# Making scale and shift together, so that the first projections of a hybrid attention block run on final inputs

## The chip, the cores and the metric

The kernel runs on one core of a Trainium2 chip. The metric is the device time of one execution, in microseconds (us), as the median of several runs. Beside the runs there is one profiled execution, with a trace of every instruction and every DMA packet. The engines are called PE (matrix products and transposes by matmul), DVE (vector), ACT (activation), POOL (GpSimd) and SP (which here only issues DMAs). DMAs can be issued from the queues of SP, ACT and POOL.

## The reference, cut to what matters

One block of a model with two branches (window attention and a gated linear recurrence). All numbers are float32. Only the first lines concern the change: 256 tokens of `x` and 256 tokens of context `ctx`, of width 2048, are normalized, scaled and shifted, and then multiplied by column groups of `w_in`.

```python
mod = silu(c) @ w_ada + b_ada                       # c: (1, 2048), w_ada: (2048, 6144)
shift, scale, gate = split(mod[:, None, :], 3, axis=-1)
mod_c = silu(c_ctx) @ w_ada + b_ada                 # the same for the context
shift_c, scale_c, gate_c = split(mod_c, 3, axis=-1)
xn = rmsnorm(x, norm_gain) * (1.0 + scale) + shift
cn = rmsnorm(ctx, norm_gain) * (1.0 + scale_c) + shift_c
... = split_columns(xn @ w_in)                      # aq ak av ag hq hff hfb hi hg ma mb
... = split_columns(cn @ w_in)
f = lb + (1 - lb) * sigmoid(z)                      # z: columns hff and hfb, forget gates
... # recurrence over hq, f, hi; window attention over aq, ak, av; gates; two output products
h = x + gate * ((sigmoid(ma + b0) * y_hgrn + sigmoid(mb + b1) * y_att) @ w_out)
return rmsnorm(h, final_norm_gain)
```

## The kernel before, in words

Every large product is done with float32 split in two parts: `wchunk` (L67) loads a piece of a weight matrix of 128 x 1024 elements into a raw buffer (`wload`, L59, issued on SP's queue), rounds it to a high part on ACT (L74, tile wh) and takes the rest on DVE (L75, tile wl). The inputs are kept likewise, as `xH` and `xL` (two halves of the tile xHL). `mm3` (L80) then makes three matmuls, high x high (L81), high x low (L82) and low x high (L83). The width 2048 is cut in KT = 16 tiles of 128, the 512 tokens (x and context) in four tiles of 128.

The opening, which the change is about, goes up to the values of the first heads:

- Small rows (c, c_ctx, biases, gains, bounds) are loaded on SP's and ACT's queues, turned by PE into columns (`cT`, `cols`).
- `turn_x` (L277) takes the sum of squares of each token tile, makes the factor 1/rms (`rstd_of`, L175, on POOL), scales the rows of X by it (L291 on ACT, L293 on DVE), and turns X in blocks of 128 x 128 on PE (L298; copied back by L300 and L302).
- `modulation(s, k, n)` (L306) makes scale (s = 1) or shift (s = 0) for n tiles from tile k on, for both c and c_ctx: `contract` (L185) runs 16 narrow matmuls (tile pa, L196) in four column strips of PE over loads of w_ada of 512 KB, ACT copies the sums (L201), PE turns them (tq, L205), DVE adds the strips (L208) and the bias (L317 or L320, L322).
- `scaled(kt)` (L332) makes xH and xL of a tile with the scale only. `first_pieces` (L368) runs the first projections on these: three groups of 256 columns of w_in (the first forget gates: C_FF, C_FB, C_FF + 256), 18 matmuls a tile, into six banks that stay open for all 16 tiles (tiles pj and pf).
- The units of scale are 2, 4, 4, 4, 2 tiles (`UNITS`, L403). In the table `plan` (L417) the steps of the next scale unit and of the shift units (`shift`, L416: three of four) are put between the pieces of the first projections.
- Behind them `shifted(kt)` (L341) makes xH and xL anew with scale and shift for 12 tiles, the six banks are copied out raw (L439, L441), and the projection HI of all four token tiles runs (`proj_tok_g`, L88). Into its steps are put the last shift unit, `shifted` for the last four tiles, and `shift_bias` (L382), which multiplies the shift with the first projections' weights, loaded again, to get what the raw banks lack (`biasF`).
- After HI, `token_values` (L753, lines L759 and L761) copies its banks out, `forget` (L478) makes the gates from the raw banks and biasF (L487 ACT, L488 DVE), and the projection HQ begins (`proj_col_x_g`, L128; its matmuls are L139 and L144).

The order on PE and SP in the opening is the order of the program (`manual_schedule`, L405); that of the other engines is fixed when the kernel is built, by priorities. Loads of the opening go to a ring of eight raw buffers (pool st), the chunks of `wchunk` to one of four, and their split parts to three pairs.

## Time and profile before

| | |
|---|---|
| median of 3 runs | 1673.35 us (1673.25 to 1674.57) |
| profiled execution, own time | 1670.86 us |
| its span in the trace | 1669.1 us |
| PE busy | 1633.2 us (98%) |
| DVE, ACT, POOL busy | 980.4, 754.0, 24.7 us |
| granted clock of PE | 0.999 |
| bytes moved by DMA | 280.45 MB, 168 GB/s over the span |

A line of a group in the profile reads: line of the kernel, engine, operation, out<-in by the program's names, shapes, count, then busy us in total and mean ns of one, then idle time of the engine just before, and what ended it. In a timeline a row is start us, duration us, engine, line, operation, operands, and in brackets the idle time before it and who ended it. Matmuls overlap, so the distance between starts is what one costs, not its duration.

### The profile page before, as it was taken

Reading aid. Unit: us, or ns where it says so; the run is one execution under the profiler, and the core shown is the slowest. Engines: PE = TensorE matmul, PEld = TensorE weight load, DVE = VectorE, ACT = ScalarE, POOL = GpSimd, SP = SyncE. Lnnn points to the kernel's source line nnn. Section 1 sums busy time; section 2 is a strip of 40 time slices with the busy share of each in tenths; the row PEclk is TensorE's granted clock in tenths of the full one; section 3 lists DMA queues with packets and bytes.
Section 4 is the critical chain, followed back from the end, with each engine's and each line's share of the span. In section 5 each row is a group of like instructions: output and inputs, shape, how many; then the busy total and the mean of one; then the engine's idle time right before and its main releaser. Section 6 shows DMA issues by size and latency. Waiting matters only on the chain.

```text
span 1669.1 us, 22846 instructions
## 1 busy us (share of the span) xinstructions
PE 1633.2 (98%) x8945; PEld 1345.0 (81%) x8945; DVE 980.4 (59%) x1533; ACT 754.0 (45%) x1125; POOL 24.7 (1%) x80
## 2 busy tenths in 40 slices
PE   5999999999999999999999999999999999999997
PEld 3657788888888888888888888888888888788887
DVE  4445577546666375754667555334677676555665
ACT  5333544324443243433445443223576777444443
POOL 1000000000000000000000000000000000000000
PEclk9999999999999999999999999999999999999999
DMA  9897654336343453434435565434545455666554
GB/s 346 309 337 259 232 168 127 114 99 213 104 128 112 132 187 107 130 106 152 141 100 171 172 196 193 141 99 132 174 137 153 138 161 158 202 202 190 180 181 139
DMA packets 182189, 280.45 MB, mean 168 GB/s; under 512 B 8961, under 2 KB 89153, under 8 KB 181313
## 3 DMA queue, kind: packets, MB, share of 16 engines
q1 hardware_dynamic: 180480, 275.70, 51.5%
q0 software_dynamic: 672, 2.11, 0.5%
q8 instruction: 70, 1.15, 0.3%
q10 hardware_dynamic: 928, 1.18, 0.2%
q14 instruction: 39, 0.31, 0.1%
HBM read 276.86 MB, written 2.10 MB: 167 GB/s over the span
## 4 chain that ended last, share of the span: by engine, by line
PE 94%; DVE 2%; DMA 1%; ACT 0%; issue 0%; SPq 0%; POOLq 0%; POOL 0%; ACTq 0%; DVEq 0%
PE pj L81 24%; PE pj L83 24%; PE pj L82 24%; PE pj L139 7%; PE pj L144 3%; PE al L567 2%; PE pa L196 1%; DMA raw<-in_w_ada_dram 1%; PE tkp L994 1%; PE sb L643 1%; DVE wl L75 0%; PE sc L83 0%; PE sc L81 0%; PE sc L82 0%; PE oba L83 0%; PE oba L81 0%
## 5 line engine op out<-in xcount | busy, mean ns | idle before, releaser
L75 DVE TENSOR_TENSOR wl<-raw,wh 128x1024 fp32r<-128x1024 f32 x396 | 484.4, 1224 | 459.1 <-ACT wh L74 458.5
L74 ACT ACTIVATE wh<-raw 128x1024 fp32r<-128x1024 f32 x396 | 419.0, 1058 | 604.4 <-PE pj L83 384.4
L83 PE MATMUL pj<-wh,xHL 128*128 128x512 f32 (+1 forms) x1024 | 397.0, 388 | 0.0
L82 PE MATMUL pj<-wl,xHL 128*128 128x512 f32 (+1 forms) x1024 | 395.8, 387 | 0.4 <-DVE wl L75 0.4
L81 PE MATMUL pj<-wh,xHL 128*128 128x512 f32 (+1 forms) x1024 | 393.1, 391 | 0.0
L81 PEld LDWEIGHTS pj<-wh,xHL 128*128 128x128 f32 x1024 | 192.3, 188 | 41.0 <-issue 3.0
L83 PEld LDWEIGHTS pj<-wh,xHL 128*128 128x128 f32 x1024 | 192.4, 188 | 39.7 <-issue 0.7
L82 PEld LDWEIGHTS pj<-wl,xHL 128*128 128x128 f32 x1024 | 192.6, 188 | 38.3 <-DVE wl L75 0.7
L81 PE MATMUL pj<-xHL,wh 128*128 128x512 f32 x480 | 191.1, 398 | 3.3 <-ACT xHL L338 3.2
L83 PE MATMUL pj<-xHL,wl 128*128 128x512 f32 x480 | 187.5, 391 | 1.8 <-DVE wl L75 1.8
L82 PE MATMUL pj<-xHL,wh 128*128 128x512 f32 x480 | 187.4, 390 | 0.0
L139 PE MATMUL pj<-xHL,wh 128*128 128x512 f32 x512 | 181.6, 398 | 1.1 <-DVE v L759 1.1
L144 PE MATMUL pj<-xHL,wl 128*128 128x256 f32 x512 | 139.9, 283 | 0.0
L139 PEld LDWEIGHTS pj<-xHL,wh 128*128 128x128 f32 x512 | 95.2, 188 | 20.8 <-DVE v L759 1.3
L81 PEld LDWEIGHTS pj<-xHL,wh 128*128 128x128 f32 x480 | 90.1, 188 | 25.7 <-ACT xHL L338 3.9
L83 PEld LDWEIGHTS pj<-xHL,wl 128*128 128x128 f32 x480 | 90.1, 188 | 21.7 <-DVE wl L75 2.6
L82 PEld LDWEIGHTS pj<-xHL,wh 128*128 128x128 f32 x480 | 90.2, 188 | 18.4 <-DVE xHL L339 0.7
L82 PE MATMUL pj<-wl,bH 128*128 128x512 f32 x256 | 100.0, 390 | 0.0
L83 PE MATMUL pj<-wh,bL 128*128 128x512 f32 x256 | 99.7, 390 | 0.0
L144 PEld LDWEIGHTS pj<-xHL,wl 128*128 128x128 f32 x512 | 96.7, 189 | 2.5
L81 PE MATMUL pj<-wh,bH 128*128 128x512 f32 x256 | 89.9, 391 | 0.1
L610 DVE TENSOR_TENSOR A<-A,X 128x512 f32<-128x512 f32 x96 | 62.0, 688 | 11.7 <-ACT qk L546 10.9
(245 smaller groups left out, 1638.3 us busy)
## 6 DMA issues: line engine op xcount, KB each, us to landing
raw<-in_w_in_dram SPq DMA_DIRECT2D x300, 512.0 KB, 3.6
raw<-in_w_ada_dram SPq DMA_DIRECT2D x96, 512.0 KB, 6.2
raw<-in_w_o_hgrn_dram SPq DMA_DIRECT2D x32, 512.0 KB, 4.1
raw<-in_w_o_attn_dram SPq DMA_DIRECT2D x32, 512.0 KB, 3.7
raw<-in_w_out_dram SPq DMA_DIRECT2D x32, 512.0 KB, 4.2
raw<-in_w_in_dram SPq DMA_DIRECT2D x32, 256.0 KB, 6.7
X<-in_x_dram SPq DMA_DIRECT2D x2, 1024.0 KB, 9.1
X<-in_ctx_dram SPq DMA_DIRECT2D x2, 1024.0 KB, 13.0
```

Source lines behind the costliest of these rows:

```text
L74: act.activation(h[:, :n], raw[:, :n], AF.Copy)
L75: dve.tensor_tensor(lo[:, :n], raw[:, :n], h[:, :n].bitcast(F32), op=ALU.subtract)
L81: pe.matmul(o, s[0], m[0], start=first, stop=False)
L82: pe.matmul(o, s[0], m[1], start=False, stop=False)
L83: pe.matmul(o, s[1], m[0], start=False, stop=last)
L139: pe.matmul(banks[i].rearrange("p (a t) -> p a t", a=2), h[:, j, cs_], xHL[:, :, kt, :T], start=kt == 0, stop=kt == KT - 1)
L144: pe.matmul(banks[i][:, :T], lo[:, j, cs_], xH[:, kt, :T], start=False, stop=False)
L196: pe.matmul(pa[32 * g: 32 * g + 32, :w], lhs[:, k0 + g, :], mv[g], start=k0 == 0, stop=k0 == KT - 4, tile_position=(0, 32 * g))
L567: pe.matmul(o, ky, mv, start=True, stop=True, tile_position=(0, 64 * c))
L610: dve.tensor_tensor(av, av, f.unsqueeze(3).to_broadcast([P, 2, n2, b]), op=ALU.mult)
L643: pe.matmul(o, wT[:, 4 * d + 2 * i + s, :], vc[:, s, (2 * p + i) * HD: (2 * p + i + 1) * HD], start=s == 0, stop=s == 1)
L994: pe.transpose(tk[:, q, :], prs[n][:, q * P: (q + 1) * P], ident)
```

## The change

Small rows go to POOL's queue, and the four loads of X come first on SP's. `turn_x` turns X unscaled; the factors 1/rms are spread over all partitions by one matmul with ones (`spread_rs`) and multiplied in later. `contract`, `scaled`, `shifted`, `shift_bias` and the raw copies are gone. `modulation(k, n)` makes scale and shift of n tiles in one go, in units of 1, 1, 2, 2, ... 2 tiles; the loads of w_ada have 128 columns for a unit of one tile and 256 for one of two. `modulate(kt)` makes the final xH and xL from X, scale, spread factors and shift. The first projections then run on these, and `forget` reads their banks directly, before HI. Between the first steps PE gets idle transposes (`rest`). The diff, cut to its core:

```diff
-    def contract(lhs, load, w, rp):
...
         with tc.high_priority(3 * PRIO):
+            for i in range(4):
+                nc.sync.dma_start(X[:, i, :], (x if i < 2 else cx)[(i % 2) * P: (i % 2 + 1) * P, :])
             nc.scalar.dma_start(cs[:, :P], cst[:, :P])
+            nc.gpsimd.dma_start(crow[0:16, :], c.rearrange("o (r p) -> (o r) p", p=P))
...
+        nc.gpsimd.dma_start(rows[0:32, :], b_ada[0:4096].rearrange("(r p) -> r p", p=P))
+        nc.gpsimd.dma_start(rows[32:48, :], rv(norm_gain))
+        nc.gpsimd.dma_start(rows2[0:32, :], lb_f.rearrange("d (r p) -> (d r) p", p=P))
+        nc.gpsimd.dma_start(rows2[32:64, :], lb_b.rearrange("d (r p) -> (d r) p", p=P))
+        nc.gpsimd.dma_start(rows2[64:80, :], rv(hg_gain))
...
+        dgx = base.tile([P, 512], F32, tag="bb", name="dgx", bufs=2)
+        ones = base.tile([P, 512], F32, tag="bb", name="onesx", bufs=2)[:, :P]
+        pool.memset(ones, 1.0)
+        rsb = fp.tile([P, 2, 512], F32, tag="acc", name="rsb")[:, 0, :]
...
-            dve.tensor_reduce(ssx[:, i: i + 1], ssy[:, i, :], mybir.AxisListType.X, ALU.add)
-            rstd_of(ssx[:, i: i + 1], D, rsx[:, i: i + 1])
-            for n in range(4):
-                blk = X[:, i, n * 512: (n + 1) * 512]
-                if n % 2:
-                    act.activation(blk, blk, AF.Copy, scale=rsx[:, i: i + 1])
-                else:
-                    dve.tensor_scalar(blk, blk, rsx[:, i: i + 1], None, op0=ALU.mult)
+            with tc.high_priority(PRIO):
+                dve.tensor_reduce(ssx[:, i: i + 1], ssy[:, i, :], mybir.AxisListType.X, ALU.add)
+                rstd_of(ssx[:, i: i + 1], D, rsx[:, i: i + 1])
+                dve.tensor_scalar(dgx[:, i * P: (i + 1) * P], ident, rsx[:, i: i + 1], None, op0=ALU.mult)
...
-        def modulation(s, k, n):
...
+        def spread_rs():
+            pr_ = ps.tile([P, 512], F32, tag="al2", name="prs")
+            pe.matmul(pr_, ones, dgx, start=True, stop=True)
+            with tc.high_priority(2 * PRIO):
+                act.activation(rsb, pr_, AF.Copy)
+        def modulation(k, n):
             w = n * P
+            nk = 1024 // w
+            pa = ps.tile([P, 512], F32, tag="al1", name="pa")
+            mv = [None] * 2
+            for k0 in range(0, KT, 4):
+                for s in (1, 0):
+                    if k0 % nk == 0:
+                        mv[s] = wload(w_ada, k0 * P, nk, (s * D + k * P,), w, st)[1][:, 0]
+                    for g in range(4):
+                        pe.matmul(pa[32 * g: 32 * g + 32, s * w: (s + 1) * w], cT[:, k0 + g, :],
+                                  mv[s][:, (k0 + g) % nk, :], start=k0 == 0 and s == 1,
+                                  stop=k0 == KT - 4 and s == 0, tile_position=(0, 32 * g))
+                yield
+            part = base.tile([P, 512], F32, tag="bb", name="part", bufs=2)
             with tc.high_priority(2 * PRIO):
+                act.activation(part[:, : 2 * w], pa[:, : 2 * w], AF.Copy)
+            yield
+            tq = ps.tile([P, 512], F32, tag="tp", name="tq")
+            for q in range(2 * n):
+                pe.transpose(tq[:, q * P: (q + 1) * P], part[:, q * P: (q + 1) * P], ident)
+            red = st.tile([P, 4, 2], F32, tag="red", name="red", bufs=2)
+            with tc.high_priority(2 * PRIO):
+                dve.tensor_reduce(red[:, : 2 * n], tq[:, : 2 * w].rearrange("p (q g r) -> p q r g", q=2 * n, g=4)
+                                  [:, :, 0:2, :], mybir.AxisListType.X, ALU.add)
+                bcol = cols[:, :32].rearrange("p (s k) -> p s k", s=2)[:, :, k: k + n].unsqueeze(3)
+                dve.tensor_tensor(mod[:, :, k: k + n, :], red[:, : 2 * n].rearrange("p (s k) r -> p s k r", s=2),
+                                  bcol.to_broadcast([P, 2, n, 2]), op=ALU.add)
+                ngc = cols[:, 32 + k: 32 + k + n].unsqueeze(2).to_broadcast([P, n, 2])
+                dve.tensor_tensor(mod[:, 1, k: k + n, :], mod[:, 1, k: k + n, :], ngc, op=ALU.mult)
-        def scaled(kt):
...
-        def shifted(kt):
...
+        rsh = halves(rsb)
+        def modulate(kt):
             xm = base.tile([P, 512], F32, tag="sm", name="xm", bufs=3)
             with tc.high_priority(2 * PRIO):
                 for i, m in enumerate(halves(xm)):
                     xv_ = X[:, 2 * i: 2 * i + 2, kt * P: (kt + 1) * P]
+                    ts = slice(i * T, (i + 1) * T)
+                    sh = mod[:, 0, kt, i: i + 1]
+                    dve.scalar_tensor_tensor(m, xv_, mod[:, 1, kt, i: i + 1], rsh[i], op0=ALU.mult, op1=ALU.mult)
+                    act.activation(xH[:, kt, ts], xm[:, ts], AF.Identity, bias=sh)
+                for i in range(2):
+                    ts = slice(i * T, (i + 1) * T)
+                    sh = mod[:, 0, kt, i: i + 1]
+                    dve.scalar_tensor_tensor(xL[:, kt, ts], xm[:, ts], sh, xH[:, kt, ts].bitcast(F32), op0=ALU.add,
+                                             op1=ALU.subtract)
...
-        def first_pieces(first, kts):
...
+        chunks = {}
+        def first_chunk(b, kt):
+            if b < 2:
+                k0, nk = (kt, 1) if kt < 2 else (kt - kt % 2, 2)
+            else:
+                k0, nk = (kt - kt % 2, 2) if kt < 4 else (kt - kt % 4, 4)
+            if (b // 2, k0) not in chunks:
+                if b < 2:
+                    chunks[0, k0] = wchunk(w_in, k0 * P, nk, (C_FF, C_FB), 256)
+                else:
+                    chunks[1, k0] = (wchunk(w_in, k0 * P, nk, C_FF + 256, 256),)
+            return chunks[b // 2, k0][b % 2], k0
+        def first_pieces(first, k, n):
+            order = [(kt, b) for kt in range(k, k + n) for b in range(3)]
+            if k + n == KT:
+                order.sort(key=lambda a: a[1])
+            for kt, b in order:
+                ch, k0 = first_chunk(b, kt)
+                proj_col_chunk(first[b], ch, k0, 512, 1, kt - k0)
                 yield
-        def shift_bias(cols0, w, q0):
...
+        def rest(n):
+            for q in range(n):
+                pe.transpose(idle[:, (q % 4) * P: (q % 4 + 1) * P], ident, ident)
-        UNITS = ((0, 2), (2, 4), (6, 4), (10, 4), (14, 2))
+        UNITS = ((0, 1), (1, 1)) + tuple((k, 2) for k in range(2, KT, 2))
         with tc.manual_schedule(engines={mybir.EngineType.PE, mybir.EngineType.SP}):
             for i in range(4):
                 turn_x(i)
+            first_chunk(0, 0)
+            idle = ps.tile([P, 512], F32, tag="o", name="idle")
+            unit = modulation(*UNITS[0])
+            rest(8)
+            take(unit, 2)
+            spread_rs()
+            rest(8)
+            take(unit, 3)
+            rest(4)
+            take(unit, 9)
+            rest(16)
             first = [(bank(), bank()), (bank(), bank()),
                      tuple(ps.tile([P, 512], F32, tag=tg, name="pf") for tg in ("o", "al2"))]
+            plan = {1: ((0, 4), (1, 1), (2, 9)), 2: ((0, 2), (2, 3), (3, 9))}
+            first_chunk(2, 0)
             for u, (k, n) in enumerate(UNITS):
                 for kt in range(k, k + n):
+                    modulate(kt)
+                after = modulation(*UNITS[u + 1]) if u + 1 < len(UNITS) else iter(())
+                for i, _ in enumerate(first_pieces(first, k, n)):
+                    take(after, dict(plan[n]).get(i, 0))
+                if u == 2:
                     bounds()
+            with tc.high_priority(2 * PRIO):
+                for b, (d, h0) in enumerate(((0, 0), (1, 0), (0, 2))):
+                    forget(first[b], d, h0, first_f[b])
             hi = proj_tok_g(w_in, C_HI, x_st, range(4))
             bv0 = result(hi)
-            take(add, 99)
```

More of the change, by code (lines that the diff above doesn't have):

```diff
@@ L302, in turn_x @@
                     dve.tensor_copy(blk, tk)
-        scl = st.tile([P, KT, 2], F32, name="scl")
-        def modulation(s, k, n):
-            w = n * P
-            def load(kt):
-                return [m[0] for m in columns(w_ada, kt, 1024 // w, (s * D + k * P,), w)]
-            red = yield from contract(cT, load, w, st)
-            bcol = cols[:, 16 * s + k: 16 * s + k + n].unsqueeze(2).to_broadcast([P, n, 2])
-            with tc.high_priority(2 * PRIO):
-                if s == 0:
-                    dve.tensor_tensor(shT[:, k: k + n, 0:2], red, bcol, op=ALU.add)
-                else:
-                    mv = scl[:, k: k + n, :]
-                    dve.tensor_tensor(mv, red, bcol, op=ALU.add)
-                    ngc = cols[:, 32 + k: 32 + k + n].unsqueeze(2).to_broadcast([P, n, 2])
-                    dve.tensor_tensor(mv, mv, ngc, op=ALU.mult)
@@ L329, in halves @@
         def halves(t):
             return [t[:, i * T: (i + 1) * T].rearrange("p (a t) -> p a t", a=2) for i in range(2)]
-        def scaled(kt):
-            with tc.high_priority(2 * PRIO):
-                for i, (h, lo) in enumerate(zip(halves(xH[:, kt, :]), halves(xL[:, kt, :]))):
-                    xv_ = X[:, 2 * i: 2 * i + 2, kt * P: (kt + 1) * P]
-                    sc = scl[:, kt, i: i + 1]
-                    act.activation(h, xv_, AF.Copy, scale=sc)
-                    dve.scalar_tensor_tensor(lo, xv_, sc, h.bitcast(F32), op0=ALU.mult, op1=ALU.subtract)
@@ L423, in block_kernel @@
                 for kt in range(k, k + n):
-                    scaled(kt)
-                after = modulation(1, *UNITS[u + 1]) if u + 1 < len(UNITS) else iter(())
-                for i, _ in enumerate(first_pieces(first, range(k, k + n))):
-                    for at_, which, steps in plan[u]:
-                        if at_ == i:
-                            take(after if which else shift, steps)
-                take(after, 9)
-                if u == 1:
-                    bounds()
-            take(shift, 99)
@@ L434, in block_kernel @@
-            for kt in range(12):
-                shifted(kt)
-            for b3, dst in zip(first, raw_f):
-                for i in range(2):
-                    if i:
-                        dve.tensor_copy(dst[:, i, :], b3[i])
-                    else:
-                        act.activation(dst[:, i, :], b3[i], AF.Copy)
-            last = modulation(0, 12, 4)
-            add = then(shift_bias((C_FF, C_FB), 256, 0), shift_bias((C_FF + 256,), 256, 4))
-            hi = proj_tok_g(w_in, C_HI, x_st, range(4))
@@ L446, in block_kernel @@
-            for k0, (g_, steps) in zip(range(0, KT, 2), ((last, 4), (last, 1), (last, 9), (add, 0), (add, 4), (add, 1),
-                                                         (add, 5), (add, 1))):
-                next(hi)
-                take(g_, steps)
-                if k0 == 4:
-                    for kt in range(12, KT):
-                        shifted(kt)
+                    modulate(kt)
+                after = modulation(*UNITS[u + 1]) if u + 1 < len(UNITS) else iter(())
+                for i, _ in enumerate(first_pieces(first, k, n)):
+                    take(after, dict(plan[n]).get(i, 0))
@@ L476, in block_kernel @@
     zeros = zero.to_broadcast([P, T])
-    def forget(banks, d, h0, F, bias=None):
-        for i in range(2):
-            sg = base.tile([P, 512], F32, tag="sm", name="sg", bufs=3)
-            if bias is None:
-                act.activation(sg, banks[i], AF.Sigmoid)
-            else:
-                for r in range(2):
-                    ts = slice(r * T, (r + 1) * T)
-                    act.activation(sg[:, ts], F[:, i, ts], AF.Sigmoid, bias=biasF[:, bias + i, r: r + 1])
-            dve.tensor_scalar(F[:, i, :], sg, lbc[:, 2 + d, h0 + i: h0 + i + 1],
-                              lbc[:, d, h0 + i: h0 + i + 1], op0=ALU.mult, op1=ALU.add)
     def pair(g, p, grp, F, banks_q):
@@ L787, in inputs @@
             output_gate((yield from proj_tok_g(w_in, C_HG, x_st, range(2))), grp)
-        F = [raw_f[2] if h0 == 2 and d == 0 else
+        F = [first_f[2] if h0 == 2 and d == 0 else
              fp.tile([P, 2, 512], F32, tag=f"F{d}", name=f"F{d}", bufs=2 - d) for d in range(2)]
```

94 lines of the change are left out of this document (17 added, 77 removed), and 4 rows, old and new, of the table plan.

## The prediction

> **What bounds the kernel now.** I read the page first, then busy time by stage, then the DMA view of the opening, then the opening instruction by instruction.
>
> ```profile
> span 1669.1 us, 22846 instructions
> PE 1633.2 (98%) x8945; PEld 1345.0 (81%) x8945; DVE 980.4 (59%) x1533; ACT 754.0 (45%) x1125; POOL 24.7 (1%) x80
> ...
> PE 94%; DVE 2%; DMA 1%; ACT 0%; issue 0%; SPq 0%; POOLq 0%; POOL 0%; ACTq 0%; DVEq 0%
> ```
> ```profile
> 0.00:13.00 13.00, 0.65 (x2) 0.36 (x2) 2.72 (x12) 3.27 (x7) 2.67 (x11) 1.00 0.71 244
> 13.00:32.00 19.00, 11.90 (x98) 9.59 (x98) 15.90 (x38) 16.39 (x35) 2.22 (x6) 1.00 1.05 390
> ...
> 60.00:100.00 40.00, 37.84 (x207) 21.84 (x206) 18.21 (x47) 15.03 (x29) 0.00 (x0) 1.00 0.97 365
> 100.00:140.00 40.00, 39.43 (x220) 28.30 (x222) 23.61 (x45) 16.72 (x26) 0.00 (x0) 1.00 0.98 361
> 140.00:200.00 60.00, 58.94 (x334) 44.20 (x326) 27.55 (x45) 23.25 (x36) 0.18 (x4) 1.00 0.63 216
> 200.00:1669.00 1469.00, 1457.40 (x7950) 1223.58 (x7949) 884.01 (x1332) 671.72 (x984) 19.58 (x59) 1.00 0.48 150
> ```
> Columns of the stage table: busy us of PE, weight load, DVE, ACT, POOL, then the granted clock, the DMA share and GB/s. From 200 us on PE is busy 1457.40 of 1469 us: nothing can absorb a shift there, so the change is worth what it moves the start of that part, which it does not touch. Before 200 us two streams are nearly full at once: PE, and the DMA engines (97% and 98% from 60 to 140 us).
>
> ```profile
> raw<-in_w_ada_dram SPq DMA_DIRECT2D x64, 512.0 KB, 7.7
> raw<-in_w_in_dram SPq DMA_DIRECT2D x32, 256.0 KB, 6.7
> X<-in_x_dram SPq DMA_DIRECT2D x2, 1024.0 KB, 9.1
> X<-in_ctx_dram SPq DMA_DIRECT2D x2, 1024.0 KB, 13.0
> rows<-in_b_ada_dram ACTq DMA_DIRECT2D x1, 16.0 KB, 2.1
> sk<-in_sink_logits_dram POOLq DMA_DIRECT2D x1, 8.0 KB, 6.2
> ```
> ```profile
> GB/s 384 386 385 385 384 386 383 387 408 410 408 410 236 25 109 303 406 397 399 390 380 408 406 289 369 377 401 381 412 408 410 403 410 406 404 414 404 412 311 51
> ```
> The second fence is the DMA rate from 100 to 140 us in slices of 1 us. Loads with 256 columns (1 KB rows) run at about 385 GB/s, loads with 512 columns (2 KB rows) at 408.
>
> The marks on PE that the sum needs:
> ```profile
> 133.67 0.39 PE L83 MATMUL pf<-xHL,wl 128*128 128x512 f32 x1
> 133.90 0.39 PE L81 MATMUL pj<-wh,xHL 128*128 128x512 f32 x1
> 135.94 0.39 PE L81 MATMUL pj<-wh,xHL 128*128 128x512 f32 x1
> 188.03 0.38 PE L205 MATMUL tq<-cs,part 128*128 128x128 f32 x2
> 188.65 0.17 DVE L392 COPY biasF<-red 128x4 f32<-128x4 f32 x1
> 188.73 0.69 DVE L759 COPY v<-pj 128x512 f32<-128x512 f32 x1
> 189.47 0.50 PE L139 MATMUL pj<-xHL,wh 128*128 128x512 f32 x1 [1.06 <-DVE v L759]
> ```
> At 133.90 the first projections (written pj or pf from xHL, wh) give way to the HI projection (pj from wh, xHL): call this moment E. Nine matmuls take 135.94 - 133.90 = 2.04 us, 0.227 us each; HI has 4 token tiles x 16 x 3 = 192, 43.6 us, but lasts 54.1 us until 188.03. Other work stands in it for 10.5 us. Then the small copy of the bias ends the opening's pool, the values are copied out, and the HQ projection starts at 189.47, which is where the untouched part begins.
>
> **The change, part by part.**
>
> *Removed from HI and behind it.* The last modulation and both bias contractions leave HI.
> ```profile
> 135.00:189.00 54.00, 9.21 (x96) 2.81 (x96) 1.00 0.72 251
> ```
> That row is L196 alone: 9.21 us of these 54. With their transposes (L205) it is the 10.5 us worked out above. The 1.44 us from 188.03 to 189.47 goes too: the value copy waits for the last reader of the opening's pool, and after the change nothing of that pool is read so late; HI's first two banks are finished 12 matmuls or more ahead of its end and can be copied under the rest. So HQ starts at E + 43.6 + 0.1, and the gain is (133.9 - E) + 10.5 + 1.3.
>
> *Removed from the DMA.* The bias contractions load the first projections' weights again: half of the 32 loads of 256 KB and 4 of 512 KB, 6.3 MB. That lies under HI, where the DMA share is 0.63 to 0.73, so it is worth nothing by itself.
>
> *Added ahead of E.* The first projections now need scale and shift of their tile. Ahead of E stand X 4.2 MB, w_ada 64 x 512 KB = 33.6 MB, first weights 6.3 MB: 44.0 MB, of which the last 0.5 MB comes behind the last w_ada load. Before, a quarter of the shift came later. Rows are 512 B in the two units of one tile (4.2 MB), else 1 KB. A row of 1 KB costs 1024/385 = 2.66 ns, one of 2 KB 2048/408 = 5.02 ns; the line through both gives 1.48 ns at 512 B, an estimate of 346 GB/s, 1.3 us lost on 4.2 MB. Bounds: 385 GB/s, or the time of a 1 KB row for half the bytes (192 GB/s, 11 us lost); the line is nearer to what the rows show.
> ```profile
> GB/s 0 0 94 58 16 34 102 132 284 437 398 425 452 397 444 418 394 470 382 481 343 392 374 384 386 382 389 384 382 388 380 407 399 407 410 410 404 410 279 358
> ...
> q1 hardware_dynamic: 5036, 9.66, 84.6%
> ...
> q1 hardware_dynamic: 2270, 5.81, 74.3%
> ...
> 0.72 0.39 SPq L247 DMA_DIRECT2D crow<-in_c_dram  x1
> 2.09 0.99 SPq L407 DMA_DIRECT2D X<-in_x_dram  x2
> ```
> The first fence line is the rate from 0 to 30 us in 40 slices; the queue of the loads had moved 9.66 MB by 30 us and 5.81 MB by 20 us. X is issued at 2.09 now and becomes the first of its queue (0.72, where the first small row stood), 1.37 us earlier: +0.5 MB, and the short rows take that back: 9.7 MB at 30 us. The other 33.8 MB at 385 GB/s take 87.8 us: the last w_ada load lands at 117.8, if the queue never runs dry. Its eight buffers hold one unit of two tiles (8 loads of 512 KB); the next unit's halves are asked for as PE consumes the two halves of this one, some 4.5 us apart, while 2.1 MB in flight last 5.5 us. So it should not run dry after the first units.
>
> *Behind the last load.*
> ```profile
> 26.62 1.93 PE L196 MATMUL pa<-raw,cT 128*32 128x256 f32 x32
> 35.25 3.64 PE L196 MATMUL pa<-raw,cT 128*32 128x512 f32 x32
> 41.68 0.60 PE L205 MATMUL tq<-cs,part 128*128 128x128 f32 x4
> 42.31 0.19 DVE L208 TENSOR_REDUCE red<-tq 128x8 f32<-128x32 f32 x1 [2.25 <-PE tq L205]
> 42.54 0.17 DVE L320 TENSOR_TENSOR scl<-red,cols 128x8 f32<-128x8 f32 x1
> 42.74 0.17 DVE L322 TENSOR_TENSOR scl<-scl,cols 128x8 f32<-128x8 f32 x1
> 42.94 3.31 ACT L338 ACTIVATE xHL<-X,scl 128x256 fp32r<-128x256 f32 x8 [3.36 <-DVE scl L322]
> 43.48 3.28 DVE L339 SCALAR_TENSOR_TENSOR xHL<-X,scl,xHL 128x256 fp32r<-128x256 f32 x8 [0.58 <-ACT xHL L338]
> ```
> The last contraction round 0.9 (a quarter of 3.64), the next piece of 6 matmuls 1.4 (the copy of the sums beside it), transposes 0.4, two more pieces 2.7, and the last unit's 36 matmuls 8.2. The two pieces cover the hand-over: reduce and two small steps 0.6, then DVE 0.41, ACT 0.41 and DVE 0.41 for a half (3.28/8 each), with the other half half a step behind: about 2.8 us against 2.7, 0.3 open; and 0.3 for the last tile. 117.8 + 0.9 + 1.4 + 0.4 + 2.7 + 0.3 + 8.2 + 0.3 = 132.0 = E by the DMA.
>
> *E by PE.* The first unit's sums follow its load: X, one piece of weights and 2.1 MB, 6.6 MB, landed by 20.7 (5.81 MB by 20 us, and 0.5 for the earlier start). Its contraction, the hand-over and the added idle transposes (36, at most 5.4 us by the 0.60 of L205's four; they stand in waits, and the last 16, up to 2.4 us, fill the first hand-over) give a first piece at 25. Two single-tile units have no piece to cover their hand-over, 2.8 us each, and the second of them waits for the next unit's load, 13.4 MB in all, until 30 + 3.7/0.385 = 39.5; with 0.9, two pieces 2.7, transposes 0.4 and 2.8 the first two-tile unit starts at 46.3. From there 14 tiles x 18 x 0.227 = 57.2, six contractions of two 256-column halves 6 x 3.8 = 22.8, transposes 2.4, openings of 0.3 seven times: E = 130.8. DMA's 132.0 is later and is taken; a period is 12.9 us by DMA (4.98 MB) and 12.7 by PE, so either may lead.
>
> *Other edits.* Turning x raw takes 16 scalings off the chain (16 of 128x512 on ACT and DVE) and adds one matmul and one copy; the turn is then done near 20 to 23 us, beside the first load. The small rows move to POOL: eight issues, landing 6.2 us after issue by the one row there is, 2.1 on ACT's queue. At half a microsecond an issue (the two of X took 0.99) the first three are in by about 9, the others by 12, and are needed at 20.7; uncovered, the difference of 6.2 and 2.1, 4.1 us, would show. POOL's rstd steps stand behind these issues, which end before the first sum of squares near 9. The forget gates move ahead of HI: six sigmoids and six scalings beside the last pieces, which finish bank by bank; uncovered, HI's first banks would wait for two of them. DVE in a unit: modulate 2 x 4 x 0.41, splits 1.5 x 1.23, small steps, 5.8 of 12.9 us.
>
> Sum: (133.9 - 132.0) + 10.5 + 1.3 = 13.7 us. The profiled run's own time is 1670.86 (span 1669.1); it becomes 1657.2. The median of the runs, 1673.35, is 2.5 higher and becomes 1659.7.
>
> *A rule against it.* The rows above, of loads with 1 KB and 2 KB rows, show 384 to 410 GB/s. The Trainium skill, "DMA: Bandwidth & Descriptors", Specifications, puts what HBM gives one core near 358 GB/s. By that figure 33.8 MB would take 94 us E would be 138.6 and the time 1666 (an estimate from that page); the trace disagrees already, so it gets a place in rival 4 and no chance beside it.
>
> **The rivals.**
> 1. PE leads, as the DMA keeps nearer to 400 than to 385 (its 2 KB slices speak for it, the row size against): E = 128, gain 17.7, 1655.6.
> 2. Hand-overs on DVE show more than 0.3.
> ```profile
> L75 DVE TENSOR_TENSOR wl<-raw,wh 128x1024 fp32r<-128x1024 f32 x26 | 31.7, 1224 | 49.9 <-ACT wh L74 49.8
> L74 ACT ACTIVATE wh<-raw 128x1024 fp32r<-128x1024 f32 x26 | 27.5, 1057 | 43.6 <-DMA raw<-in_w_in_dram 31.9 <-issue 6.0 <-PE pj L139 3.3
> ...
> PE pj L81 <- ACT xHL L338: 3.2, 2, 2.4
> ```
> DVE's order is fixed, and a split of 1.22 ahead of the reduce delays it. One such in each of seven units gives 7 x (1.2 - 0.3 of slack) = 6.3 us: E = 138, 1666. For it: DVE gets four steps a tile where it had two before the matmuls; against: before, PE waited for L338 twice, 3.2 us in all.
> 3. Slower: the same place, with two splits and the ACT half (1.06) of another ahead of each hand-over, 3.5 us each. Seven cost 7 x 3.2 = 22 us: E = 154, 1682. It decides from 1.95 + 0.3 us open per unit on, where the 13.7 are gone. Against it: DVE's 5.8 of 12.9 us leave room, and splits are asked for a unit early.
> 4. Loads are slower: 512 B rows at half rate cost 10 us more (1669.5, about no change); if all ran at the mean of the stage from 60 to 100 us, 365 GB/s, 33.8 MB take 92.6, 4.8 us more (1664.5). That stage has a gap of PE's making, so its mean is a low bound, and nothing in the rows speaks for the half rate.
>
> **How the numbers follow.** What a measurement here can tell from no change is 0.2%, 3.3 us. Forecast 0.54; rival 1 0.14; rival 2 0.14; rival 3 0.09; rival 4 0.09 (two thirds of it no change, as it touches that bound). Faster: 0.54 + 0.14 + 0.14 + 0.02 = 0.84, less 0.02 for a rival 2 of larger size: 0.82; the same 0.08; slower 0.10. Range: rival 1 and 2.0 below it, 1653.5, to rival 2 and 1.5 above it, 1667.5; rivals 3 and the dear half of 4 are left out, 0.15.
>
> **What would show it.** Right: HI starts (first pj from wh, xHL) near 132 and lasts 43.6 without other matmuls; HQ starts near 175.8 with no wait for a value copy; 1 KB loads at 385 GB/s and a DMA share above 0.95 from 10 to 117; first piece near 25. Wrong: E past 147; PE waiting for xHL by microseconds in every unit; DMA slices well under 346 in the first 25 us; or the part behind HQ longer than the 1479.6 us it has now.

## Result: slower, where a gain was forecast

The changed kernel takes 1685.55 us (median of 4 runs, 1682.71 to 1685.84), the kernel before 1673.96 (4 runs beside them, 1673.25 to 1674.81). The ratio is 1.0065, 95% interval 1.0048 to 1.0083: 11.6 us slower, where 13.7 us faster was forecast and 1667.5 was the upper end of the range. The profiled run's own time is 1685.84 us.

From the page of the changed kernel: the span, the busy time of each engine, and the clock granted to TensorE in 40 slices.

```profile
span 1684.1 us, 23285 instructions
...
PE 1645.1 (98%) x9201; PEld 1359.7 (81%) x9201; DVE 968.9 (58%) x1512; ACT 739.1 (44%) x1094; POOL 30.5 (2%) x88
...
PEclk9899999999999999999999999999999999999999
```

PE is busy 11.9 us longer than before (1633.2), with some of it at a lower clock: the second slice (42 to 84 us) reads 8. Next, PE's own timeline of the changed kernel, cut to the marks that the prediction used: first piece, first unit of two tiles, first matmul of HI (the moment E), first of HQ.

```profile
27.81 0.50 PE L81 MATMUL pj<-xHL,wh 128*128 128x512 f32 x1 [0.37 <-ACT xHL L338]
...
51.27 0.80 PE L81 MATMUL pj<-xHL,wh 128*128 128x512 f32 x1 [4.57 <-ACT xHL L338]
...
161.22 0.39 PE L81 MATMUL pj<-wh,xHL 128*128 128x512 f32 x1
...
204.74 0.39 PE L139 MATMUL pj<-xHL,wh 128*128 128x512 f32 x1
```

| step | forecast | changed kernel |
|---|---|---|
| first piece | 25 | 27.81 |
| first unit of two tiles | 46.3 | 51.27 |
| E | 132.0 | 161.22 |
| HI, from E to HQ | 43.6 + 0.1 | 43.52, no wait at HQ |
| behind HQ | 1479.6 | 1684.1 - 204.74 = 1479.4 |

Everything behind E came as forecast, 12.1 us cheaper than before (55.57 from E to HQ before, 43.52 now). The whole loss is E, 29.2 us later than forecast; 24.3 of them fall between 51.27 and 161.22, in seven units of two tiles (110.0 us where 85.7 were forecast), 3.5 us a unit.

The stage table of the changed kernel (start:end, length, then busy us of PE, weight load, DVE, ACT, POOL, granted clock, DMA share, GB/s): first from the first pieces to E, then exactly two units, from one late start to the next but one.

```profile
27.50:161.20 133.70, 114.81 (x831) 75.27 (x832) 50.16 (x115) 36.69 (x62) 0.18 (x4) 0.91 0.84 285
101.42:133.78 32.36, 29.44 (x208) 18.77 (x209) 11.23 (x27) 7.67 (x14) 0.00 (x0) 0.90 0.89 301
```

Neither PE nor the DMA is full: PE idles 18.9 us, the transfers run at 285 GB/s, and the clock is 0.91. Two units take 32.36 us, where 25.8 (2 x 12.9) was forecast. What PE waits for in the first 200 us (us in total, times, longest):

```profile
PE pj L81 <- ACT xHL L338: 14.4, 7, 4.6
...
PE pj L82 <- DVE xHL L342: 3.9, 6, 0.9
```

That is the hand-over: the modulated tile's high part from ACT (L338) and its low part from DVE (L342). Why they come late stands in the three queues between 120 and 135 us. Timelines of SP, ACT and DVE (in brackets the idle time before, and what ended it), then PE's:

```profile
120.97 2.10 SPq L64 DMA_DIRECT2D raw<-in_w_ada_dram  x4
123.17 0.84 SPq L64 DMA_DIRECT2D raw<-in_w_in_dram  x1
```
```profile
127.18 0.60 ACT L309 ACTIVATE part<-pa 128x512 f32<-128x512 f32 x1 [2.63 <-PE pa L303]
131.47 1.06 ACT L74 ACTIVATE wh<-raw 128x1024 fp32r<-128x1024 f32 x1 [3.69 <-DMA raw<-in_w_in_dram]
132.44 1.69 ACT L338 ACTIVATE xHL<-xm,mod 128x256 fp32r<-128x256 f32 x4
```
```profile
129.74 1.67 DVE L337 SCALAR_TENSOR_TENSOR xm<-X,mod,rsb 128x256 f32<-128x256 f32 x4
132.56 1.22 DVE L75 TENSOR_TENSOR wl<-raw,wh 128x1024 fp32r<-128x1024 f32 x1 [1.15 <-ACT wh L74]
133.71 1.66 DVE L342 SCALAR_TENSOR_TENSOR xHL<-xm,mod,xHL 128x256 fp32r<-128x256 f32 x4
```
```profile
105.10 3.38 PE L303 MATMUL pa<-raw,cT 128*32 128x256 f32 x32
...
111.36 1.93 PE L303 MATMUL pa<-raw,cT 128*32 128x256 f32 x32
...
133.78 0.50 PE L81 MATMUL pj<-xHL,wh 128*128 128x512 f32 x1 [1.93 <-ACT xHL L338]
135.03 0.51 PE L82 MATMUL pj<-xHL,wh 128*128 128x512 f32 x1 [0.74 <-DVE xHL L342]
```

The first half's xm is ready 0.4 us after 129.74, and ACT has nothing else to do, but its next instruction is the split of the third weight group (C_FF + 256), which waits 3.69 us for its load. SP asked for that load at 123.17, behind four w_ada loads, which themselves wait for PE to consume the half before them; it landed 8.2 us later. Only then does ACT make the high part, and DVE, for the same reason, the low part. This repeats in every second unit of two tiles (new weights of that group come every four tiles); the other units lose less. And behind four of the five waits above 1.7 us PE runs at half clock for a while: the 32 matmuls at 105.10 take 3.38 us, the same 32 at 111.36 take 1.93.

The longest wait, 4.57 us ahead of the first unit of two tiles (51.27), has the same cause. This unit takes new weights of the third group too, and of ACT's four hand-over steps the last two stand behind their split. Its load was asked for at 42.88 and landed 7.20 us later. SP's and ACT's timelines:

```profile
42.88 1.19 SPq L64 DMA_DIRECT2D raw<-in_w_in_dram  x1
```
```profile
47.88 0.91 ACT L338 ACTIVATE xHL<-xm,mod 128x256 fp32r<-128x256 f32 x2 [2.27 <-DVE xm L337]
50.19 0.63 ACT L74 ACTIVATE wh<-raw 128x512 fp32r<-128x512 f32 x1 [1.40 <-DMA raw<-in_w_in_dram]
50.72 0.89 ACT L338 ACTIVATE xHL<-xm,mod 128x256 fp32r<-128x256 f32 x2
```

### The profile page after: what moved, and what is told of

It is laid out like the page before. It is cut to its first block, busy times and chain, and to the rows that moved or that the text cites. A ratio compares the mean times of both kernels' runs of the same rounds, so it can differ in the third digit from the quotient of the medians.

```text
span 1684.1 us, 23285 instructions
## 1 busy us (share of the span) xinstructions
PE 1645.1 (98%) x9201; PEld 1359.7 (81%) x9201; DVE 968.9 (58%) x1512; ACT 739.1 (44%) x1094; POOL 30.5 (2%) x88
## 4 chain that ended last, share of the span: by engine, by line
PE 92%; DVE 3%; DMA 3%; ACT 1%; issue 1%; SPq 0%; POOLq 0%; ACTq 0%; POOL 0%; DVEq 0%
PE pj L81 23%; PE pj L82 23%; PE pj L83 23%; PE pj L139 7%; PE pj L144 3%; DMA raw<-in_w_in_dram 2%; PE al L528 2%; PE pa L303 2%; PE tkp L952 1%; PE sb L604 1%; DVE wl L75 1%; PE sc L83 0%; PE sc L81 0%; PE sc L82 0%; PE oba L83 0%
## 5 line engine op out<-in xcount | busy, mean ns | idle before, releaser
L75 DVE TENSOR_TENSOR wl<-raw,wh 128x1024 fp32r<-128x1024 f32 (+1 forms) x398 | 484.4, 1217 | 486.0 <-ACT wh L74 485.5
L74 ACT ACTIVATE wh<-raw 128x1024 fp32r<-128x1024 f32 (+1 forms) x398 | 419.5, 1054 | 653.1 <-PE pj L83 414.0
L82 PE MATMUL pj<-wl,xHL 128*128 128x512 f32 (+1 forms) x1024 | 395.6, 386 | 0.4 <-DVE wl L75 0.4
L82 PEld LDWEIGHTS pj<-wl,xHL 128*128 128x128 f32 x1024 | 192.5, 188 | 38.4 <-DVE wl L75 0.7
L81 PE MATMUL pj<-xHL,wh 128*128 128x512 f32 x480 | 195.0, 406 | 14.4 <-ACT xHL L338 14.4
L82 PE MATMUL pj<-xHL,wh 128*128 128x512 f32 x480 | 190.6, 397 | 3.9 <-DVE xHL L342 3.9
L139 PE MATMUL pj<-xHL,wh 128*128 128x512 f32 x512 | 181.2, 397 | 0.0
L82 PEld LDWEIGHTS pj<-xHL,wh 128*128 128x128 f32 x480 | 91.4, 190 | 24.5 <-DVE xHL L342 7.1
L82 PE MATMUL pj<-wl,bH 128*128 128x512 f32 x256 | 99.9, 390 | 0.0
```

The lines of the kernel that those rows point to most:

```text
L74: act.activation(h[:, :n], raw[:, :n], AF.Copy)
L75: dve.tensor_tensor(lo[:, :n], raw[:, :n], h[:, :n].bitcast(F32), op=ALU.subtract)
L81: pe.matmul(o, s[0], m[0], start=first, stop=False)
L82: pe.matmul(o, s[0], m[1], start=False, stop=False)
L139: pe.matmul(banks[i].rearrange("p (a t) -> p a t", a=2), h[:, j, cs_], xHL[:, :, kt, :T], start=kt == 0, stop=kt == KT - 1)
```

## The experiments

Two theories were tried against each other. *Order*: what costs is a step that stands ahead of the hand-over in ACT's and DVE's fixed order; the clock only follows. *Clock*: the waits are small, and what costs is the half clock that they bring on. To move single instructions, the first kernel writes out the opening's order for ACT and DVE by hand; the others change that kernel or one another, and the last but one the kernel before. In the written-out kernels the same steps stand a little lower in the code: matmuls L82 to L84, splits L75 and L76, hand-over L356 (ACT) and L360 (DVE). The diffs are shortened: in the runs some of these lines are chosen by a constant. The comparison runs of the kernel before had a median of 1673.1 to 1673.2 us.

**e0_written_out.** The changed kernel with ACT and DVE in the hand-written order too, as near to the recorded order as it goes (the third unit's loads and the bounds stand a little otherwise).

```diff
+            with tc.manual_schedule(engines={mybir.EngineType.Activation, mybir.EngineType.DVE}):
                 for u, (k, n) in enumerate(UNITS):
...
+                    load_half(*nxt, 0)
+                    if fresh: load_chunk(2, k)      # the third group, behind the first half
+                    load_half(*nxt, 1)
+                    modulate(list(range(k, k + n)), (lambda: split_chunk(2, k)) if fresh else None)
```

> The changed kernel with the order of ACT and DVE in the opening written out as the trace of the changed kernel shows it (two steps of the third unit and the bounds stand a little otherwise). A base for the next runs. Every theory expects 1685 us, +-4, and the first projections' end near 161 us.

Measured 1678.68 us (1676.06 to 1680.7), ratio 1.003 [1.0019, 1.0041], E = 154.36. It missed the changed kernel's time by 6.9 us: the kinds of waits are the same, but most are shorter (one is longer, 5.02 us ahead of the first unit of two tiles). Which of the small differences makes up the 6.9 was not taken apart. It is the base for what follows.

**e1_clock.** Idle transposes at the end of seven units, so that PE does not stand still.

```diff
-            RESTS = ()
+            RESTS = (0, 10, 20, 6, 24, 6, 20, 6)
```

> As the base, with 6 to 24 idle transposes at the end of each unit, so that PE does not fall idle in the hand-overs; nothing moved on ACT, DVE or SP. Theory 'clock' (PE's half clock after each idle stretch is the loss by itself, 16.9 us of it): 1669 us, end of the first projections near 145. Theory 'order' (the split of the third weight group stands ahead of the hand-over and waits for its load, and that chain of 16 us from a unit's first contraction to the next unit does not go through PE): only the units without such a split gain, three times 3 us: 1676 us. Theory 'loads' (row length limits the rate): 1685.

Measured 1676.26 us (1674.73 to 1677.25), ratio 1.0017 [1.0008, 1.0027], E = 151.45. The same stretch in e0_written_out and then in e1_clock:

```profile
27.50:130.00 102.50, 89.56 (x691) 57.05 (x690) 36.45 (x88) 25.46 (x44) 0.00 (x0) 0.92 0.99 334
```
```profile
27.50:130.00 102.50, 93.70 (x783) 65.68 (x782) 38.95 (x92) 26.70 (x46) 0.00 (x0) 0.98 1.01 345
```

The clock is back (0.98) and only 2.4 us with it. Both theories had reckoned from a base of 1685, *clock* with 16 us to gain and *order* with 9. *Clock* falls: PE is warm, busy with transposes that nothing reads, while it waits for the same hand-over.

**e2_split_behind.** The third group's split stands behind the hand-over's four steps.

```diff
                 for kt in group: scale_(kt)
-                between()
                 for kt in group: high(kt)
                 for kt in group: low(kt)
+                between()
```

> As the base, with only the split of the third weight group moved behind the hand-over on ACT and DVE (four times in all); same loads in the same order, same PE order. Theory 'order': the units after such a split shorten from 16 to about 13.5 us and idle stretches above 1.5 us go, and with them most of the half clock: end of the first projections near 143, 1667 us. Theory 'clock': the hand-over keeps its other idle time, so half of the 16.9 stay, 1676. Theory 'loads': 1685.

Measured 1665.18 us (1664.46 to 1666.16), ratio 0.9952 [0.9937, 0.9967], E = 141.68. One split moved takes 13.5 us off the base, to 1.8 us below the 1667 that *order* expected (*clock*: 1676). As the base is itself 6.3 us under the 1685 reckoned with, the total decides less than the stage. The changed kernel, e0_written_out and e2_split_behind in the same stretch:

```profile
64.00:129.00 65.00, 57.98 (x422) 37.50 (x421) 23.91 (x58) 16.89 (x28) 0.00 (x0) 0.92 0.92 311
```
```profile
64.00:129.00 65.00, 60.62 (x438) 39.36 (x437) 26.24 (x65) 17.51 (x30) 0.00 (x0) 0.95 0.98 332
```
```profile
64.00:129.00 65.00, 64.02 (x516) 42.58 (x514) 28.81 (x67) 20.85 (x35) 0.18 (x4) 1.00 1.05 369
```

PE does 516 matmuls where it did 438 in e0_written_out and 422 in the changed kernel, at full clock without a single filling transpose. *Order* stands.

**e3_all_order.** Besides, the hand-over tile by tile (xm, high, low of one tile, then of the next), and the third group's load asked for ahead of the next unit's w_ada halves.

```diff
-            for group in [kts]:
+            for group in [[kt] for kt in kts]:
...
+                            if fresh: load_chunk(2, k)
                             load_half(*nxt, 0)
-                            if fresh: load_chunk(2, k)
```

> As the run before, and also hand-over tile by tile on DVE (the first tile is complete before the second begins) and the third group's load asked for ahead of the next unit's first half. Theory 'order': idle per unit 0.3 to 0.5 us, period 12.9 by the DMA: end of the first projections at 135 to 138, 1660 to 1663 us. Theory 'loads': 1680 or more. Theory 'clock': no idle, no half clock: as 'order'.

Measured 1663.93 us (1662.62 to 1665.32), ratio 0.9944 [0.9929, 0.9959], E = 138.19. PE's timeline: the same contraction in three successive units, and the last unit's start:

```profile
90.41 1.93 PE L314 MATMUL pa<-raw,cT 128*32 128x256 f32 x32
...
103.40 1.93 PE L314 MATMUL pa<-raw,cT 128*32 128x256 f32 x32
...
116.28 1.93 PE L314 MATMUL pa<-raw,cT 128*32 128x256 f32 x32
...
128.38 0.49 PE L82 MATMUL pj<-xHL,wh 128*128 128x512 f32 x1 [0.40 <-ACT xHL L356]
129.63 0.50 PE L83 MATMUL pj<-xHL,wh 128*128 128x512 f32 x1 [0.76 <-DVE xHL L360]
```

The period is 12.99 and 12.88 us: the forecast's 12.9. E and the median lie 0.2 and 0.9 us above what *order* expected at most. What is left is ahead of it (the two single-tile units) and at the last unit, where HI's first split stands ahead of the hand-over in the same manner.

**e5_load_early.** e0_written_out with the load alone asked for earlier; the split stays ahead of the hand-over. It tells the wait for the load from the length of the split.

```diff
+                            if fresh: load_chunk(2, k)
                             load_half(*nxt, 0)
-                            if fresh: load_chunk(2, k)
```

> e0_written_out with one edit: the third weight group's load is asked for on SyncE's queue ahead of the next unit's first four w_ada loads instead of behind them. Its split still stands ahead of the hand-over on ScalarE and VectorE. 'Wait in the order' (the price is the wait of that split for its load, 52.3 us over 12 waits of ScalarE in the changed kernel, which holds the hand-over back): the wait goes, the split's own 1.06 and 1.22 us stay ahead of the hand-over, so each of the four units that take new weights loses some 1 to 2 us instead of 3 to 4; HI starts at 142 to 147 us instead of 154.4, median 1666 to 1671. 'Splits' (rival 3 of the prediction as it was priced: the length of the splits themselves, not the wait): nothing but the moment of the transfer changes, HI at 152 to 155, median 1676 to 1679.

Measured 1670.88 us (1668.52 to 1672.34), ratio 0.9987 [0.9977, 0.9996], E = 144.88. ACT's timeline, then PE's:

```profile
91.24 1.06 ACT L75 ACTIVATE wh<-raw 128x1024 fp32r<-128x1024 f32 x1 [2.55 <-PE pj L83]
92.20 1.69 ACT L356 ACTIVATE xHL<-xm,mod 128x256 fp32r<-128x256 f32 x4
```
```profile
93.15 0.49 PE L82 MATMUL pj<-xHL,wh 128*128 128x512 f32 x1 [0.39 <-ACT xHL L356]
94.40 0.50 PE L83 MATMUL pj<-xHL,wh 128*128 128x512 f32 x1 [0.76 <-DVE xHL L360]
```

The split no longer waits for its load but for its buffer, which PE's last piece of the unit before frees; ACT stands still for 2.55 us, nearly all of it before the first xm is there (91.1), and PE's waits in the hand-over are down to 0.39 + 0.76 us. *Wait in the order* stands here; *splits* (1676 to 1679) falls. Two whole units, from one such start to the next, in e0_written_out, e5_load_early and (from contraction to contraction) e3_all_order:

```profile
100.00:130.49 30.49, 28.09 (x209) 18.04 (x209) 11.24 (x26) 7.69 (x14) 0.00 (x0) 0.94 0.98 330
```
```profile
93.15:121.01 27.86, 26.48 (x209) 17.58 (x209) 11.23 (x26) 7.68 (x14) 0.00 (x0) 1.00 1.02 355
```
```profile
90.41:116.28 25.87, 25.87 (x210) 17.61 (x209) 11.63 (x27) 7.73 (x14) 0.00 (x0) 1.00 1.09 384
```

About the same 209 matmuls, and 32.36 us of them in the changed kernel. So the 6.5 us that it loses in two units part into 1.9 for the small differences of e0, 2.6 for the wait for the load with the half clock behind it, and 2.0 for the split's place and the tile-wise hand-over. By where PE loses them: 2.9 idle, 3.6 at half clock (29.44 busy against 25.87).

How the last 4.6 part depends on what is moved first. In e2_split_behind, where the split goes behind the hand-over and its load stays late, two units take 26.72 us:

```profile
65.64:92.36 26.72, 26.35 (x209) 17.65 (x209) 12.84 (x34) 9.22 (x16) 0.00 (x0) 1.00 1.08 377
```

So the split's place alone brings 3.8, and the early load with the tile-wise hand-over only 0.9 more. Over the whole kernel the early load alone is worth 7.8 us, the move alone 13.5: the load's wait costs only because the split stands ahead of the hand-over, and the split's own length costs there as well.

**e4_last_unit.** e3_all_order with HI's first split behind the last hand-over, and 8 idle transposes before the first unit of two tiles.

```diff
-            RESTS = ()
+            RESTS = (0, 8, 0, 0, 0, 0, 0, 0)
...
+                    else:
+                        hi0 = wchunk(w_in, 0, 2, C_HI, 512)
-            hi = proj_tok_g(w_in, C_HI, x_st, range(4))
+            hi = proj_tok_g(w_in, C_HI, x_st, range(4), hi0)
```

> e3_all_order with two further edits: the split of HI's first weights stands behind the last hand-over in ScalarE's and VectorE's order instead of ahead of it, and 8 transposes that nothing reads fill TensorE's idle 2.1 us before the first unit of two tiles. 'Order' (each gap of TensorE in this stage is a step that stands behind another one on ScalarE or VectorE; the clock only follows): the last hand-over's 0.40 + 0.76 us and what the following half clock costs go, about 1.5 us, and the half-clocked start of the first unit of two tiles gives at most 1 us more, if the loads had not set that unit's end anyway: HI starts near 136 us instead of 138.2, median 1661 to 1662.5. 'Loads' (the w_ada and w_in transfers set the stage once the hand-overs are covered): the gap before HI only moves, HI stays at 137.5 to 138.5, median 1663 to 1664.

Measured 1661.28 us (1660.34 to 1662.76), ratio 0.9929 [0.9914, 0.9944], E = 136.30, as *order* has it. From 80 us to E, PE's idle times of any length are two of 0.29 and 0.43 us.

**e6_rows_back.** e4_last_unit with the eight small rows on ACT's queue instead of POOL's.

```diff
-            nc.gpsimd.dma_start(crow[0:16, :], c.rearrange("o (r p) -> (o r) p", p=P))
+            nc.scalar.dma_start(crow[0:16, :], c.rearrange("o (r p) -> (o r) p", p=P))
...
-        nc.gpsimd.dma_start(rows2[64:80, :], rv(hg_gain))
+        nc.scalar.dma_start(rows2[64:80, :], rv(hg_gain))
```

> e4_last_unit with one edit: the eight small rows are asked for on ScalarE's queue again instead of GpSimd's, on which they landed 5.5 to 6.7 us after they were issued. 'Rows late': the first piece of the first projections starts 1 to 2 us earlier than the 26.8 us of e3_all_order, and the chain of loads behind it follows in part: 0.5 to 2 us less than e4_last_unit. 'Rows hidden' (the first w_ada loads set the first piece): within 0.5 us of e4_last_unit, or up to 1 us slower, since their issues now stand ahead of ScalarE's first work.

Measured 1667.46 us (1666.51 to 1668.82), ratio 0.9965 [0.9953, 0.9976], E = 143.13: 6.2 us slower, which neither theory had. ACT's timeline and PE's:

```profile
5.90 0.32 ACTq L245 DMA_DIRECT2D rows<-in_b_ada_dram  x1
...
12.80 0.32 ACTq L249 DMA_DIRECT2D rows<-in_hgrn_norm_gain_dram  x1
13.15 1.28 ACT L268 ACT_TABLE_LOAD   x1 [13.15 <-DMA rows<-in_norm_gain_dram]
14.44 0.63 ACT L268 ACTIVATE junk<-X 128x512 f32<-128x512 f32 x1
```
```profile
34.33 0.51 PE L82 MATMUL pj<-xHL,wh 128*128 128x512 f32 x1 [0.46 <-ACT xHL L356]
```

The last row is issued at 12.80 us, so ACT's first sum of squares starts at 14.44 instead of 5.92, the turn of x waits for ACT's copies (4.79 us in one place), and the first piece comes at 34.33 instead of 26.84. On ACT's queue beside X's loads the rows land no sooner either (3.5 to 8.0 us after issue), and the issues hold up the engine that has the sums of squares to do. They stretch to 12.80 us because, as far as the times show, they wait for earlier transfers: the eight take 3.4 us together, but each of the last five starts within 0.1 us of the landing of an earlier one (the last at 12.80, where the row asked for at 5.90 lands, 6.9 us later). SP's next issues wait likewise:

```profile
SPq L64 <- DMA X<-in_ctx_dram: 4.6, 2, 2.3
SPq L64 <- DMA X<-in_x_dram: 3.9, 1, 3.9
```

The first w_ada load is thus asked for at 12.98 us instead of 3.92. The bytes are less behind (303 GB/s over the first 20 us against 318), but what of the 6.2 us is ACT's lateness and what SP's was not taken apart. In the kernel before, where X's loads stand behind three small ones, ACT's last row is issued at 4.95.

**e8_rows_alone.** The kernel before with that part alone: X first on SP's queue, small rows on POOL's.

```diff
-            nc.sync.dma_start(crow[0:16, :], c.rearrange("o (r p) -> (o r) p", p=P))
+            nc.gpsimd.dma_start(crow[0:16, :], c.rearrange("o (r p) -> (o r) p", p=P))
...
-        nc.scalar.dma_start(rows[0:32, :], b_ada[0:4096].rearrange("(r p) -> r p", p=P))
+        nc.gpsimd.dma_start(rows[0:32, :], b_ada[0:4096].rearrange("(r p) -> r p", p=P))
```

> The kernel before with one part of the change alone: X's four loads stand first on SyncE's queue and the eight small rows go by GpSimd's queue; the turn of x, the one-tile units, the projections on raw x and the correction rows stay as they were. 'Rows' (as e6_rows_back showed, rows on ScalarE's queue behind X's loads hold that engine and the w_ada loads up): X lands some 4 us earlier and with it the norms and the first turned tile, but the first projections of the kernel before wait for the turned and scaled x, which also needs the mean square of each half, so the first piece comes 1 to 4 us earlier; the end of the w_ada loads sets the stage anyway: 1670 to 1673 us. 'Nothing without the raw turn' (the parts are worth something only together): 1672.5 to 1674 us.

Measured 1670.86 us (1669.03 to 1672.4), ratio 0.9986 [0.9976, 0.9995]: 2.3 us, inside the 0.2% that counts as no change. The first piece comes 1.0 us earlier, at 31.04 instead of 32.02; HI starts at 134.50 instead of 133.90 in the profiled runs, so the gain in the median is not seen there.

**e7_units_of_two.** e3_all_order with HI's first split behind the last hand-over and units of two tiles throughout.

```diff
-        UNITS = ((0, 1), (1, 1)) + tuple((k, 2) for k in range(2, KT, 2))
+        UNITS = tuple((k, 2) for k in range(0, KT, 2))
...
+                        split_chunk(0, 1)
+                        modulate([0, 1])
```

> e3_all_order with HI's first split behind the last hand-over, and units of 2, 2, 2 ... tiles instead of 1, 1, 2, 2 ...: the two single-tile units with their hand-overs in the open (idle 2.1 us and more before each, and the half clock behind) are gone, the first piece waits for the loads of two tiles. 'Loads': the first piece comes some 5.5 us later (near 32 us), but the loads run on under it and TensorE's first eight pieces of two tiles make up for it at 12.7 us a unit against 12.9 of the loads; HI starts at 133 to 136 us, median 1658 to 1661. 'TensorE': work that the single-tile units did before 46 us is now done later, 2 x 6 us of it, and is not made up: HI at 139 to 143, median 1664 to 1668.

Measured 1658.3 us (1658.27 to 1658.36), ratio 0.9911 [0.9896, 0.9925]: the best of all, 14.9 us faster than the kernel before. PE's timeline, with the starts of the first pieces, of HI and of HQ:

```profile
33.53 0.50 PE L82 MATMUL pj<-xHL,wh 128*128 128x512 f32 x1 [1.28 <-ACT xHL L356]
...
133.96 0.39 PE L82 MATMUL pj<-wh,xHL 128*128 128x512 f32 x1
...
177.48 0.39 PE L140 MATMUL pj<-xHL,wh 128*128 128x512 f32 x1
```

The first piece comes 6.7 us later than in e4_last_unit and HI 2.3 us earlier: the loads ran on meanwhile, and from 33.53 to HI PE waits once, for 0.5 us. *TensorE* (work put off is lost) falls, *loads* stands. Yet E only comes back to where it was in the kernel before (133.90): the whole gain lies behind E.

| kernel | us | E |
|---|---|---|
| before | 1673.96 | 133.90 |
| changed | 1685.55 | 161.22 |
| e0_written_out | 1678.68 | 154.36 |
| e1_clock | 1676.26 | 151.45 |
| e5_load_early | 1670.88 | 144.88 |
| e6_rows_back | 1667.46 | 143.13 |
| e2_split_behind | 1665.18 | 141.68 |
| e3_all_order | 1663.93 | 138.19 |
| e4_last_unit | 1661.28 | 136.30 |
| e7_units_of_two | 1658.30 | 133.96 |
| e8_rows_alone | 1670.86 | 134.50 |

The time is a median, E comes from the one profiled run. Time less E is 1523.5 to 1526.0 us in all of them but the kernel before (1540.1) and e8_rows_alone (1536.4), in which other work still stands in HI: over 27 us the time follows E. The profiled run of the kernel before took 1670.86 us, 3.1 less than its median; with that time it has 1537.0 behind E, and the gain of e7_units_of_two is 12.5 instead of 14.9.

## Why the prediction was wrong

**Right, behind E.** HI in 43.52 us without foreign matmuls (43.6), HQ with no wait for a value copy, 1479.4 behind it (1479.6). The 10.5 + 1.3 us were there in full: 55.57 - 43.52 = 12.05. The bias contractions' weights, worth nothing by themselves, fit that.

**Right, the limit of the loads.** A period of 12.9 us at about 385 GB/s is what e3_all_order reaches (384 GB/s in the stretch above, and in e7_units_of_two from 46 to 72 us). The estimate of 346 GB/s for rows of 512 B came near: 342 measured from 14 to 27 us in the changed kernel, where nearly all loads are such. The eight small rows landed 5.5 to 6.5 us after issue, about the 6.2 taken; they were needed later than that. The Trainium skill's 358 GB/s ("DMA: Bandwidth & Descriptors", Specifications) is passed here too: 384 measured, with one core at work.

**The step that failed: the hand-over, "2.8 us against 2.7, 0.3 open".** It summed the durations of the hand-over's own steps and took it that they start when their data is there. The order on ACT and DVE is fixed, and the step ahead of them waited for a load. Of the unit's hand-over 0.3 us was to stay open; per unit 3.5 us more than that came out (in the two units taken apart 1.5 of it as idle time and 1.8 as half clock). This is the place of rival 3, and its total (1682 us, seven units at 3.5) is close to the 1685.55 measured, but only in part for its reason: it priced split durations (1.22, 1.22 and 1.06), and taking the wait for the split's load away while the splits stay where they are brings 7.8 us (e5_load_early). The splits' own length is a part too: with them behind the hand-over 13.5 us come back (e2_split_behind). The argument that set its chance at 0.09, "splits are asked for a unit early", holds for the first two weight groups; the third group's load is issued behind four w_ada loads of the next unit, and these wait for PE. The row that bore on it was in the prediction: splits of before waited 31.9 us for their loads (L74 <-DMA). They cost little there (PE waited for L338 twice, 3.2 us in all); the question left out was which step stands behind them after the change.

**The step left out: the half clock.** "PE leads" and the 12.7 us of PE a unit assumed a clock of 1.00. The changed kernel had 0.91 from 27.5 to 161.2 us. It was a consequence and not a cause of its own: with the waits gone, the clock is 1.00 (e2_split_behind, 64 to 129 us), and with the clock alone restored in e0_written_out only 2.4 us come back (e1_clock).

**Mis-sized, the start.** First piece 27.81 instead of 25, first unit of two tiles 51.27 instead of 46.3. The two hand-overs in the open cost 2.12 and 4.57 us where 2.8 each were allowed. The second is the failed step again: it is 5.02 us in e0_written_out, but 2.14 with the split behind it (e2_split_behind) or its load early (e5_load_early). For the first piece the forecast let the idle transposes stand in waits; in the changed kernel PE never waits from 17.31 to 25.2 us, and 20 of them, some 2.7 us, stand in that stretch. What the first piece would be without them was not tried. e7_units_of_two shows that the kernel is better without the one-tile units. Its 1658.3 us lies 1.4 from the 1659.7 forecast, but that is luck: E is 133.96 there, not 132.0, and part of the difference to the kernel before is that kernel's spread.

**Seen from one side, the rows' queue.** The forecast priced the rows' move by when they land. Its 2.1 us for ACT's queue was one row, asked for ahead of X; the three asked for behind X's first loads took 7.7 to 8.5 us there in the kernel before, so POOL's queue cost nothing by that measure. e6_rows_back shows its other side: with the eight issues on ACT, waiting for earlier transfers, ACT's first sum of squares starts 8.5 us later and the kernel takes 6.2 us longer.

**Open.** The 6.9 us between the changed kernel and e0_written_out; the order of ACT and DVE in the changed kernel differs from the written one in several small places, and none was tried alone. The experiments change the written-out kernel; that the 6.9 us are of the same kind is likely by the waits, and not shown.

## What to carry to other kernels

Where an engine works in a fixed order, sum what stands ahead of the critical step with the moment its data comes, not with its duration: a step off the critical path that waits for a load puts that wait in front of everything behind it. Follow such a load back to its own issue: here it stood in a queue behind loads that waited for the very engine it was holding up. Moving the step behind the hand-over was worth more here than bringing its load forward (13.5 us against 7.8). And price an issue by what it waits for and by what its engine has to do at that moment, not only by when the data lands.

## What the runs showed of the hardware

Half clock can follow two idle times of less than 0.8 us each. In the changed kernel PE idles 0.79 and 0.75 us around one matmul of 0.5 at 150.30 to 151.55, and from 152.68 matmuls of 0.39 us take 0.63, until 155.67:

```profile
150.30 0.50 PE L81 MATMUL pj<-xHL,wh 128*128 128x512 f32 x1 [0.79 <-ACT xHL L338]
151.55 0.50 PE L82 MATMUL pj<-xHL,wh 128*128 128x512 f32 x1 [0.75 <-DVE xHL L342]
...
152.68 0.63 PE L83 MATMUL pj<-xHL,wl 128*128 128x512 f32 x1
...
155.67 0.48 PE L81 MATMUL pj<-xHL,wh 128*128 128x512 f32 x1
```

In e5_load_early, 0.39 and 0.76 us around one matmul bring none. The single-tile unit's 2.12 us brought half clock in e0_written_out (0.91 from 27 to 46 us) and none in the changed kernel (1.00 in the same stretch). The Trainium skill, "TensorE: Matmul & The Clock Gate", Part 1: The HAM clock gate, states a free-running window of about 3.4 us, of which an idle one halves the clock. A free-running window agrees with the same wait going both ways; that a window must be idle throughout does not agree with two idle times of less than 0.8 us.

DMA issues hold back what stands behind them on their engine: in e6_rows_back eight small issues, 0.3 to 0.9 us each with waits between them, keep ACT's first work until 13.15 us. The Trainium skill, "Trainium Kernel Development and Optimization", Key Constraints, states that issuing from several engines saves only the sequencer's issue time. Here more than the issues' own 3.4 us was at stake: the waits between them came on top, and the kernel took 6.2 us longer.
